# A hybrid diffusion layer: normed activations kept in DRAM as f32 rows and split again on reload, their block sums made at other times, query columns first

## The chip, the cores and the metric

The kernel runs on one core of a Trainium2 chip. The metric is device time in microseconds (us) of one execution. The engines are called as the profile calls them: PE (TensorE matmul) with PEld (its weight loads), DVE (VectorE), ACT (ScalarE), POOL (GpSimd) and SP (SyncE, which issues most DMAs here); ACT issues some stores too.

## The reference

One layer over 2048 latent tokens (a 32x64 grid) and 256 context tokens, width 1024, in f32:

```python
h_lat = _rmsnorm(x, norm_g) * (1.0 + scale) + shift      # ctx in the same way with shift_c, scale_c
na_q, na_k, na_v, na_g, r_q, r_k, r_v, r_g = _split_proj(h_lat @ w_in)      # 8 groups of 512 columns
# the context tokens go through the same weights
o_na  = neighbourhood attention, 8 heads of 64, 8x16 window plus all context keys, one softmax
y_na  = o_na * silu(na_g)
o_ret = bidirectional retention, 4 heads of 128, chunks of 128, states started from the context
y_ret = head_rmsnorm(o_ret) * silu(r_g)
x = x + gate * (concat([y_na, y_ret]) @ w_out)
return _rmsnorm(x, final_norm_g)
```

Below, h is the normed and modulated input of the projection, `h_lat` or `h_ctx`.

## The kernel before

f32 products are made on PE from pairs: each operand is split into `hi` (a cast to fp32r by ACT) and `lo` (the rest, a subtraction on DVE or POOL), and three matmuls (hi·hi, hi·lo, lo·hi) are added up in PSUM. This holds for h and for the weights. A weight group is 256 columns of `w_in`: two raw halves `st` of 128x1024, split by `w_split` into `whi` and `wlo`, for which the pool `wa` has two buffers of each.

h lies transposed in SBUF, in four latent blocks of 512 tokens and a context block of 256: `blk[b]` is a pair (hi, lo). Blocks 0 and 1 are in the pool `hx`, 2 and 3 in `hy`, the context in `cp` (`chi`, `clo`). SBUF doesn't hold all of h besides what later stages need, so blocks are written to DRAM (`hS`) and read back.

The work goes by in stages. Times are microseconds from the start of the span in the profiled execution:

- 0 to 163: x and the ada weights are loaded and the modulation made. Then `window(b)` for the five blocks: the NA keys of the block (`u_k`, PE line L354) are projected while a list of numbers, `PLAN`, interleaves the preparation of the following blocks. `prep_ab` makes raw h in place (`raw[i]`, 256 tokens each), `prep_hl` splits it.
- 163 to 197: six context units (four of `CTXU`, two of `u_v`), each of 48 matmuls of 256 columns (L365). Ahead of each a weight group is split.
- 197 to 244.6, values 1: eight `u_v` units for blocks 0 and 1. At every fifth `yield` of the units a step of `h_sums` runs.
- 244.6 to 368.7, Strassen 1 (L626): for blocks 0 and 1 the columns of `SETS` (two gate groups of each head group, `SETS` 1536, 1792, 3584, 3840, and the NA queries 0 and 256) by Strassen's form, seven products instead of eight, 12 matmuls of 512 columns each. It needs sums of h blocks, the tiles `T` from `h_sums`, and sums of weight blocks from `w_sums`. `w_set` is one column group in four steps; after each step, `hooks` and what is left of the weight sums (`mine`, `ahead`) are called.
- 368.7 to 423.7, values 2: `u_v` for blocks 3 and 2, which are reloaded from `hS`, with `h_sums` for this pair.
- 423.7 to 557.2, Strassen 2 with the products `wo_mul` of the output weights (tile `g`, stored to `woS`).
- 557.2 to 1050: more projections (retention values, keys, queries), from 592 as fill between the neighbourhood attention tiles; blocks 0 and 1 are reloaded meanwhile through the list `dmas`, one entry for one step of the fill.
- 1050 to 1391: the rest of the retention and the output projection.

Each engine takes its instructions in the order in which the program writes them, and so do the DMA queues of SP and ACT. Order is set by the Python code alone: who writes a step at which yield. `h_sums` has ten steps: `first`, `second` and `third` (two each, on 128x1024 pairs) and `fourth` (four, on 128x512). In `first` DVE subtracts hi parts, POOL lo parts (`e`), DVE adds both, ACT casts and DVE makes the low part. `spill_step` writes a piece of 512 KB of hi or lo to `hS`: 32 pieces, 16 of them in windows 2 and 3 on SP and 16 in Strassen 1 through `hooks`.

Of the kernel before, what the change touches and what calls it, by code (L numbers as in the profile page):

```python
# [18 lines left out]
P = 128  # L19
# [63 lines left out]
def hybrid_kernel(ctx: ExitStack, tc: tile.TileContext, a: dict, out: bass.AP):  # L83
# [15 lines left out]
    hS = [[dram.tile([P, KC * 512], F32, name=f"hS{b}_{hl}") for hl in range(2)] for b in range(4)]  # L99
# [146 lines left out]

    def prep_first(k):
        for i in range(2):
# [17 lines left out]
    def prep_hl(i, u):  # L266
        hi, lo = sub_dst(i)
        x, ks = raw[i][u], slice(u * KH, (u + 1) * KH)
        nc.scalar.copy(hi[:, ks, :], x)
        eng = nc.vector if LOV[i] >> u & 1 else nc.gpsimd  # L270
        eng.tensor_tensor(lo[:, ks, :], x, f(hi[:, ks, :]), ALU.subtract)  # L271
# [199 lines left out]
    SETS = (1536, 1792, 3584, 3840, 0, 256)  # L471
# [10 lines left out]
    spill = [(b, hl, k) for b in (2, 3, 0, 1) for hl in range(2) for k in range(0, KC, 2)]  # L482

    def spill_step():
        if spill:
            b, hl, k = spill.pop(0)
            nc.sync.dma_start(hS[b][hl][:, k * 512:(k + 2) * 512], f(blk[b][hl])[:, k:k + 2, :].rearrange("p k t -> p (k t)"))

    def window(b):
        units = [u_k(w01, 512 + 256 * g, ct, b) for g in range(2) for ct in range(2)]  # L490
        left = [KC] * 4
        for n, u in enumerate(STEPS if b == 0 else [u for u in range(4) for _ in range(KC)]):
            if b == 4 and n == 16:
                wr.append(w_split(wr[2]))
            next(units[u])
            left[u] -= 1
            run_acts(32 * b + n)
            if b in (2, 3) and n % 4 == 3:
                spill_step()
            if not left[u]:  # L500
                for _ in units[u]:
                    pass
                tick()
# [4 lines left out]
    def reload_parts(b):  # L508
        blk[b] = (hx.tile([P, KC, 512], F32R, name="hhi"), hx.tile([P, KC, 512], F32R, name="hlo"))
        return [(f(blk[b][hl])[:, k:k + 2, :].rearrange("p k t -> p (k t)"), hS[b][hl][:, k * 512:(k + 2) * 512])  # L510
                for k in range(0, KC, 2) for hl in range(2)]

    def h_sums(T, A, B):
# [42 lines left out]
        def fourth(k):  # L556
            if k == 0:
                tile_(1, "hhi")
                T.extend(tl[n] for n in (1, 3, 2, 4))
                tl["o"] = env["st"].tile([P, 2, 512], F32, name="o3", bufs=1)  # L560
            d = tl["o"][:, k % 2, :]
# [46 lines left out]
    def plain_next(res):  # L608
        def p1():
            res.append(w_split(wcur.pop(0), lo=1))  # L610

        return [None, p1, None, None, None, None]

    def w_set(c0, W, T, A, B, mine, ahead, hooks):
# [18 lines left out]
        def fin(o, ct, b):  # L633
# [5 lines left out]
            g = f(o)[:, 1, :]  # L639
# [4 lines left out]
        def step(n):  # L644
            tick()
            for fn in mine[4 + n:5 + n] + ahead[n:n + 1]:
                if fn:
                    fn()
            if hooks:
                for h in hooks.pop(0):  # L650
                    h()
# [21 lines left out]
        od, xd = out_tile()  # L673
# [3 lines left out]
        fin(od, 1, B)  # L677
# [38 lines left out]
    def unit(g, nsp=0):  # L716
        for _ in g:
            pass
        tick()
        for _ in range(nsp):  # L720
            spill_step()
# [10 lines left out]
    def values(ws, bb, hs, hook):  # L732
        vu = [(w, c0, tp) for w, c0 in zip(ws, (1024, 1280)) for b in bb for tp in (2 * b, 2 * b + 1)]
        y = 0
        for n, (w, c0, tp) in enumerate(vu):
            for _ in u_v(w, c0, tp):
                y += 1
                if hs and y % 5 == 0:
                    hs.pop(0)()
            tick()  # L740
            if n == 4:
                W, mine = w_sums(wcur.pop(0))
            if n > 3 and n < 7:
                mine[n - 4]()
            if n in hook:
                hook[n]()
        while hs:
            hs.pop(0)()
        mine[3]()
        return W, mine  # L750

    load_w()
    w0 = wr[3]
    for c0, u in CTXU:
# [8 lines left out]
    T = []  # L763
    W, mine = values((w0, w1), (0, 1), h_sums(T, 0, 1), {})
    wo_open()

# [4 lines left out]
    hooks = [[spill_step] if n < 16 else [] for n in range(24)]  # L771
# [3 lines left out]
    hooks[21].insert(0, lambda: take(2))  # L775
    mid = []
    strassen(T, 0, 1, W, mine, hooks, mid)
    w0, w1 = mid + [w_split(wcur.pop(0), lo=1)]
    load_w()
    load_w()  # L780
    T = []
    W, mine = values((w0, w1), (3, 2), h_sums(T, 2, 3), {1: lambda: wo_gate(7), 7: wo_row})
# [36 lines left out]
    def reload(b):  # L819
        for d in reload_parts(b):  # L820
            dmas.extend([None, None, d])

# [75 lines left out]
    def fill(n):  # L898
        for _ in range(n):
            if dmas:  # L900
                d = dmas.pop(0)
                if d:
# [643 lines left out]
```

## Time and profile before

Three runs took 1393.6, 1394.55 and 1390.81 us, the median is 1393.6. The profiled execution took 1392.92 us, its span is 1391.1 us, and the mean clock granted to PE was 0.984 of the full one.

| engine | busy us | share of span | instructions |
|---|---|---|---|
| PE | 1323.0 | 95% | 8236 |
| DVE | 840.3 | 60% | 1434 |
| POOL | 627.1 | 45% | 585 |
| ACT | 591.0 | 42% | 1239 |

The DMA moved 295.64 MB, 196.57 read and 97.52 written in HBM.

A row of the timeline reads: start and duration in us, engine, line of the kernel, operation, output and input tile, shape, count, and in brackets the idle time before it and what ended it. A row of waits reads: engine, operation and line that waited, what it waited for, us in total, times, the longest. A row of the windows has the busy time (and count) of PE, PEld, DVE, ACT and POOL in a stretch, the granted clock, the DMA's share and its GB/s.

### The profile page before, as it was taken

Reading aid. Unit: us, or ns where it says so; the run is one execution under the profiler, and the core shown is the slowest. Engines: PE = TensorE matmul, PEld = TensorE weight load, DVE = VectorE, ACT = ScalarE, POOL = GpSimd, SP = SyncE. Lnnn points to the kernel's source line nnn. Section 1 sums busy time; section 2 is a strip of 40 time slices with the busy share of each in tenths; the row PEclk is TensorE's granted clock in tenths of the full one; section 3 lists DMA queues with packets and bytes.
Section 4 is the critical chain, followed back from the end, with each engine's and each line's share of the span. In section 5 each row is a group of like instructions: output and inputs, shape, how many; then the busy total and the mean of one; then the engine's idle time right before and its main releaser. Section 6 shows DMA issues by size and latency. Waiting matters only on the chain.

```text
span 1391.1 us, 23111 instructions
## 1 busy us (share of the span) xinstructions
PE 1323.0 (95%) x8236; PEld 1157.6 (83%) x8236; DVE 840.3 (60%) x1434; ACT 591.0 (42%) x1239; POOL 627.1 (45%) x585
## 2 busy tenths in 40 slices
PE   6989999899998999899999999999999899999997
PEld 2477999688886777898899899889999789888886
DVE  5787247565676465377766777776663634344445
ACT  4454332333323334265555545456652234433332
POOL 4452434445426556255445434465433145454342
PEclk9999999999989999999999999999999999999999
DMA  9547864596975657976686899967627888555533
GB/s 310 176 166 273 287 193 111 150 351 215 349 222 145 210 189 248 297 200 185 171 225 176 214 262 271 258 181 207 174 87 249 261 289 276 184 169 167 159 114 129
DMA packets 231765, 295.64 MB, mean 213 GB/s; under 512 B 17633, under 2 KB 172385, under 8 KB 230626
## 3 DMA queue, kind: packets, MB, share of 16 engines
q1 hardware_dynamic: 200322, 237.79, 57.9%
q10 hardware_dynamic: 31328, 56.37, 11.3%
q8 instruction: 66, 1.08, 0.3%
q14 instruction: 49, 0.40, 0.1%
HBM read 196.57 MB, written 97.52 MB: 211 GB/s over the span
## 4 chain that ended last, share of the span: by engine, by line
PE 46%; DVE 4%; DMA 2%; ACT 2%; issue 1%; POOL 1%; SPq 0%; ACTq 0%; POOLq 0%; DVEq 0%
PE mm L1390 11%; PE mm L365 10%; PE sS L950 5%; PE mm L354 4%; PE tr L977 3%; PE po L998 3%; PE tr L979 2%; PE mm L1113 2%; PE po L1000 2%; DMA v<-rvS 1%; PE mm L1302 1%; PE mm L1301 1%; PE mm L1300 1%; PE mm L1281 1%; DVE xt L1358 1%
## 5 line engine op out<-in xcount | busy, mean ns | idle before, releaser
L365 PE MATMUL mm<-whi,hhi 128*128 128x256 f32 x768 | 227.1, 296 | 6.3 <-ACT o L440 5.8
L365 PE MATMUL mm<-whi,hlo 128*128 128x256 f32 x768 | 219.6, 286 | 3.3 <-DMA hlo<-hS 3.3
L365 PE MATMUL mm<-wlo,hhi 128*128 128x256 f32 x768 | 219.0, 285 | 0.0
L981 ACT CAST pt<-tr 128x640 fp32r<-128x640 f32 (+1 forms) x128 | 95.6, 747 | 169.6 <-PE tr L979 168.3
L987 DVE TENSOR_TENSOR pt<-tr,pt 128x640 fp32r<-128x640 f32 (+1 forms) x128 | 113.9, 890 | 76.9 <-ACT pt L981 75.6
L365 PEld LDWEIGHTS mm<-whi,hhi 128*128 128x128 f32 x768 | 148.6, 194 | 7.1 <-ACT o L440 6.0
L970 POOL TENSOR_SCALAR sp<-sp,stt 128x640 f32<-128x640 f32 (+2 forms) x128 | 103.0, 807 | 112.8 <-DVE stt L969 71.8
L365 PEld LDWEIGHTS mm<-whi,hlo 128*128 128x128 f32 x768 | 148.9, 194 | 4.4 <-DMA hlo<-hS 4.3
L365 PEld LDWEIGHTS mm<-wlo,hhi 128*128 128x128 f32 x768 | 148.4, 193 | 0.0
L959 DVE CUSTOM_DVE_ANT_0 sp<-sS,nb 128x640 f32<-128x640 f32 (+2 forms) x128 | 105.5, 824 | 29.3 <-PE sS L950 22.3
L964 ACT ACTIVATE sp<-sp,stt 128x640 f32<-128x640 f32 (+2 forms) x128 | 107.4, 839 | 18.9 <-DVE stt L959 17.8
L338 POOL TENSOR_TENSOR wlo<-st,whi 128x256 fp32r<-128x256 f32 (+1 forms) x79 | 83.7, 1073 | 68.8 <-ACT whi L336 67.1
L354 PE MATMUL mm<-hhi,whi 128*128 128x512 f32 x256 | 107.6, 420 | 0.0
L354 PE MATMUL mm<-hlo,whi 128*128 128x512 f32 x256 | 101.8, 398 | 5.4 <-DVE hlo L271 2.3
L950 PE MATMUL sS<-k,q 128*128 128x256 f32 (+3 forms) x512 | 98.8, 315 | 5.2 <-DVE stt L959 4.9
L354 PE MATMUL mm<-hhi,wlo 128*128 128x512 f32 x256 | 101.8, 398 | 0.2 <-DVE wlo L338 0.2
L626 PE MATMUL mm<-hhi,whi 128*128 128x512 f32 x336 | 98.4, 395 | 1.2 <-POOL whi L580 1.0
L1390 PE MATMUL mm<-wor,y 128*128 128x512 f32 x384 | 95.6, 398 | 1.0 <-DVE xt L1399 1.0
L1399 DVE TENSOR_TENSOR xt<-mm,xt 128x512 f32<-128x512 f32 x64 | 43.8, 686 | 86.1 <-PE mm L1390 86.1
L950 PEld LDWEIGHTS sS<-k,q 128*128 128x128 f32 x512 | 82.9, 188 | 11.6 <-DVE stt L959 7.7
L1390 PE MATMUL mm<-won,y 128*128 128x512 f32 x336 | 89.9, 406 | 0.0
L1390 PEld LDWEIGHTS mm<-wor,y 128*128 128x128 f32 x384 | 69.9, 188 | 17.1 <-issue 3.5
(254 smaller groups left out, 3098.3 us busy)
## 6 DMA issues: line engine op xcount, KB each, us to landing
st<-in_w_in_dram SPq DMA_DIRECT2D x64, 512.0 KB
q<-qS SPq DMA_DIRECT2D x64, 256.0 KB
k<-kS SPq DMA_DIRECT2D x16, 576.0 KB
kS<-o SPq DMA_DIRECT2D x16, 512.0 KB
hS<-hhi SPq DMA_DIRECT2D x16, 512.0 KB
hS<-hlo SPq DMA_DIRECT2D x16, 512.0 KB
vB<-o SPq DMA_DIRECT2D x64, 128.0 KB
qS<-o ACTq DMA_DIRECT2D x16, 512.0 KB
```

The lines of the kernel that those rows point to most:

```text
L338: eng.tensor_tensor(l, r, f(h), ALU.subtract)
L354: nc.tensor.matmul(pm[:, :n], ww[:, k, cs], h[:, k, :], start=(k == 0 and i == 0), stop=(k == KC - 1 and i == 2))
L365: nc.tensor.matmul(pm[:, t * WG:(t + 1) * WG], h[:, k, o:o + P], ww[:, k, :], start=(k == 0 and i == 0), stop=(k == KC - 1 and i == 2))
L626: nc.tensor.matmul(pm, ww[:, k, :], hh[:, k, :], start=(k == 0 and i == 0), stop=(k == KH - 1 and i == 2))
L950: nc.tensor.matmul(o, hd["q"][i][:, hl, j * P:(j + 1) * P], k, start=(hl == 0), stop=(hl == 1))
L959: nc.vector.tensor_tensor_reduce(T["sp"][:, :n], T["s"], nbz[big][:, o:o + n], -1.0, 3e38, ALU.add, ALU.min, T["st"][:, 0:1])
L964: nc.scalar.activation(sp[:, :n], sp[:, :n], AF.Exp, bias=st[:, 0:1], scale=-1.0, accum_out=st[:, 1:2])
L970: nc.gpsimd.tensor_scalar(sp[:, :n], sp[:, :n], st[:, 2:3], 0.0, ALU.mult, ALU.add)
L981: nc.scalar.copy(pt[:, :ng_ + 2, 0, :], tr[:, :ng_ + 2, :])
L987: nc.vector.tensor_tensor(pt[:, :n, 1, :], tr[:, :n, :], f(pt)[:, :n, 0, :], ALU.subtract)
L1390: nc.tensor.matmul(pm, yy[:, k, :], ww[:, k, sl], start=(k == 0 and i == 0), stop=(k == 3 and i == 2))
L1399: nc.vector.tensor_tensor(xts[t][:, sl], pm, xts[t][:, sl], ALU.add)
```

## The change

`hS` holds raw h, f32, one copy (8 MB) instead of hi and lo (16 MB). It is written in the windows from the raw tiles, one piece at every odd step. On reload a block is the raw rows in the `lo` tile, and `re_split` makes `hi` (ACT) and then `lo` in place (DVE or POOL). In Strassen 1 nothing is stored to `hS` any more. In the attention the splits of blocks 0 and 1 stand in `dmas` as calls.

For the first pair `h_sums` stays (its `fourth` with a tile `e` made on POOL), but its steps begin in the context units: `pump` calls one step at every eighth yield, which is the last yield of a unit, ahead of the unit's evacuation. For the second pair `h_sums_raw` makes the sums from raw rows as far as it can, with the splits between them: `open_b` in the sixth group of Strassen 1, nine steps at every fourth yield of values 2. In values 2 each block is used with both weight groups before the next (before: each weight group with both blocks), the second group is split after unit 0, and the weight sums are made after units 5 to 7 (in values 1 after 3 to 5). In `SETS` the two query groups come first; a gate group takes one `o` tile fewer.

```diff
-    hS = [[dram.tile([P, KC * 512], F32, name=f"hS{b}_{hl}") for hl in range(2)] for b in range(4)]
+    hS = [dram.tile([P, KC, 512], F32, name=f"hS{b}") for b in range(4)]
...
+    def spill_step():
+        if spill:
+            i, u = spill.pop(0)
+            o = i % 2 * 256
+            nc.sync.dma_start(hS[i // 2][:, u * KH:(u + 1) * KH, o:o + 256], raw[i][u])
...
-    SETS = (1536, 1792, 3584, 3840, 0, 256)
+    SETS = (0, 256, 1536, 1792, 3584, 3840)
...
-            if b in (2, 3) and n % 4 == 3:
+            if n % 2:
                 spill_step()
...
+        return [(f(blk[b][1])[:, k:k + 2, :], hS[b][:, k:k + 2, :]) for k in (0, 4, 2, 6)]
+
+    def re_split(b, ks, eng):
+        hi, lo = blk[b]
+        nc.scalar.copy(hi[:, ks, :], f(lo)[:, ks, :])
+        eng.tensor_tensor(lo[:, ks, :], f(lo)[:, ks, :], f(hi)[:, ks, :], ALU.subtract)
...
+        def open_b():
+            tile_(0, "hhi", F32)
+            for c in range(2):
+                V.tensor_tensor(d(c), lb[:, pairs(c + 2), :], lb[:, pairs(c), :], ALU.subtract)
+            for n in (0, 2, 1, 3):
+                re_split(B, pairs(n), (V, G)[n // 2])
...
+        def raw_a(m):
+            for n in (m, m + 2):
+                re_split(A, pairs(n), (V, G)[n // 2])
+            low(4, m, d(m), (G, V)[m])
...
+        return open_b, [a, b, lambda: first(0), lambda: first(1), c_, lambda: raw_a(0), lambda: raw_a(1), lambda: last(0), lambda: last(1)]
...
-            V(d, d, bl[:, k, :], ALU.add)
-            V(d, d, al[:, k, :], ALU.subtract)
+            V(d, d, e, ALU.add)
...
-    def unit(g, nsp=0):
+    pump = dict(y=0, every=8, q=[])
+
+    def unit(g):
         for _ in g:
-            pass
+            pump["y"] += 1
+            if pump["q"] and pump["y"] % pump["every"] == 0:
+                pump["q"].pop(0)()
...
+    pump["q"] = h_sums(T, 0, 1)
     for c0, u in CTXU:
         wn = w_split(wcur.pop(0), lo=1)
...
+    W, mine = values(vunits([(mid, 1024, 3), (w1, 1280, 3), (mid, 1024, 2), (w1, 1280, 2)]),
+                     {0: [lambda: w1.append(w_split(wcur.pop(0), lo=1)), load_w, load_w], 1: [lambda: wo_gate(7)], 7: [wo_row]}, 5)
...
+        dmas.extend([None] * 4)
+        dmas.extend(lambda k=k: re_split(b, slice(k, k + 1), nc.gpsimd) for k in (0, 1, 4, 5, 2, 3, 6, 7))
```

How this moves instructions is shown at three places. In the rows a line number is that of the kernel named, so the same operation has another number after the change. The first place is ACT in the context units, before; `whi` is a weight group's cast, `o<-mm` the evacuation of a unit:

```order
L336 CAST whi<-st 128x1024 x2
L434 ACTIVATE o<-mm 128x512
L336 CAST whi<-st 128x1024 x2
L434 ACTIVATE o<-mm 128x512
L150 DMA rkS_77<-o 128x2x256
L336 CAST whi<-st 128x1024 x2
L440 COPY o<-mm 128x512
```

And after:

```order
L348 CAST whi<-st 128x1024 x2
L599 CAST hlo<-hhi 128x1024
L446 ACTIVATE o<-mm 128x512
L348 CAST whi<-st 128x1024 x2
L599 CAST hlo<-hhi 128x1024
L446 ACTIVATE o<-mm 128x512
L150 DMA rkS_77<-o 128x2x256
L348 CAST whi<-st 128x1024 x2
L599 CAST hhi<-hhi 128x1024
L452 COPY o<-mm 128x512
```

The cast of a block sum (L599) now stands ahead of each evacuation, and so ahead of the next weight group's casts.

The second place is SP in windows 2 and 3, before; `kS` are stored keys, `in_ctxT_dram` is the context's load:

```order
L150 DMA kS_64<-o 256x1x512
L487 DMA hS_0_91<-hhi 128x1024 x2
L150 DMA kS_61<-o 256x1x512
L487 DMA hS_0_91<-hhi 128x1024
L176 DMA st<-in_ctxT_dram 128x4x256 x2
```

And after:

```order
L253 DMA hS_89<-hhi 128x4x256 x3
L150 DMA kS_64<-o 256x1x512
L150 DMA kS_61<-o 256x1x512
L253 DMA hS_90<-chi 128x4x256 x2
L176 DMA st<-in_ctxT_dram 128x4x256 x2
L150 DMA kS_62<-o 256x1x512
```

The two pieces of raw h in `chi` (tokens 1536 to 1791) are stored ahead of the context's load.

The third place is DVE at the end of Strassen 1, before; L669 to L675 are the last sums of `w_set`, L636 the low part of a query tile, L338 that of a weight group, L533 to L525 steps of `h_sums`:

```order
L669 TENSOR_TENSOR o_3022<-mm,o_3022 128x512
L636 SCALAR_TENSOR_TENSOR o<-o 128x512
L674 TENSOR_TENSOR o_3022<-mm,o_3022 128x512
L675 TENSOR_TENSOR o<-mm,e 128x512
L636 SCALAR_TENSOR_TENSOR o_3022<-o_3022 128x512
L636 SCALAR_TENSOR_TENSOR o<-o 128x512
L338 TENSOR_TENSOR wlo<-st,whi 128x1024
L533 TENSOR_TENSOR hhi<-hhi 128x1024
L535 TENSOR_TENSOR hhi<-hhi 128x1024
L525 TENSOR_TENSOR hlo<-hhi,hlo 128x1024
```

And after, where L742 to L748 are those last sums, L544 and L520 are `open_b`, L537, L558, L564 and L565 the steps `a`, `b` and `first`, and L416 the evacuation of a value unit:

```order
L742 TENSOR_TENSOR o_2995<-mm,o_2995 128x512
L544 TENSOR_TENSOR hhi<-hlo 128x1024 x2
L520 TENSOR_TENSOR hlo<-hlo,hhi 128x1024 x2
L747 TENSOR_TENSOR o_2995<-mm,o_2995 128x512
L748 TENSOR_TENSOR o<-mm,e 128x512
L537 TENSOR_TENSOR hlo<-hhi,hlo 128x1024
L558 TENSOR_TENSOR hhi<-hhi,hlo 128x1024 x2
L416 TENSOR_TENSOR o<-mm,o 128x4x128
L350 TENSOR_TENSOR wlo<-st,whi 128x1024
L564 TENSOR_TENSOR o_3152<-hhi,hlo 128x1024
L565 TENSOR_TENSOR o_3152<-o_3152,hlo 128x1024
```

The splits and sums of the second pair stand ahead of the last two sums of Strassen 1 and of the second weight group.

More of the change, by code (lines that the diff above doesn't have):

```diff
@@ L245, in ab @@
         return scl[u][:, q, s:s + 1], mod[u][:, 0, q, s:s + 1]
+    spill = []
+    def spill_step():
[3 more added lines that the diff above has]
+            nc.sync.dma_start(hS[i // 2][:, u * KH:(u + 1) * KH, o:o + 256], raw[i][u])
     def prep_first(k):
+        if k == KC - 1:
+            spill.extend((i, u) for i in range(2) for u in range(2))
         for i in range(2):
@@ L269, in prep_hl @@
         nc.scalar.copy(hi[:, ks, :], x)
+        if i < 8:
+            spill.append((i, u))
         eng = nc.vector if LOV[i] >> u & 1 else nc.gpsimd
@@ L480, in load_w @@
             wcur.append(w_raw(wseq.pop(0)))
[L482 to L487, printed above, removed]
     def window(b):
@@ L769, in take, with take_a @@
             nc.sync.dma_start(*d)
-    hooks = [[spill_step] if n < 16 else [] for n in range(24)]
+    T2, raws = [], []
+    def take_a():
+        take(2)
+        raws.extend(h_sums_raw(T2, 2, 3))
+    hooks = [[] for n in range(24)]
     for k in range(7):
```

111 lines of the change are left out of this document (72 added, 39 removed).

## The prediction

> **What bounds the kernel now.** I read the page first: busy shares, then the granted clock.
>
> ```profile
> PE 1323.0 (95%) x8236; PEld 1157.6 (83%) x8236; DVE 840.3 (60%) x1434; ACT 591.0 (42%) x1239; POOL 627.1 (45%) x585
> PEclk9999999999989999999999999999999999999999
> ```
>
> TensorE (PE) is busy 95% of 1391.1 us and nearly always at full clock, and the change keeps its matmuls. So it can only move the stalls. Those I read in PE's waits, then stage by stage in the windows (columns: stretch, length, busy time and count of PE, PEld, DVE, ACT, POOL, clock, DMA share, GB/s).
>
> ```profile
> PE mm L626 <- ACT wlo L579: 8.4, 3, 4.8
> PE mm L365 <- ACT o L440: 5.8, 1, 5.8
> PE mm L626 <- POOL wlo L580: 4.3, 6, 1.3
> PE mm L365 <- DMA hlo<-hS: 3.3, 4, 0.9
> ...
> 163.00:197.00 34.00, 33.36 (x277) 32.96 (x276) 12.45 (x7) 13.02 (x16) 20.59 (x9) 1.00 0.74 237
> 197.00:244.60 47.60, 47.60 (x399) 47.60 (x398) 35.65 (x29) 12.23 (x18) 16.55 (x9) 1.00 0.45 113
> 244.60:368.70 124.10, 119.68 (x506) 96.52 (x505) 75.68 (x91) 43.18 (x75) 60.98 (x43) 0.97 0.75 251
> 368.70:423.70 55.00, 51.19 (x385) 49.67 (x385) 41.46 (x34) 14.31 (x19) 22.80 (x10) 0.91 0.77 254
> 423.70:557.20 133.50, 124.00 (x510) 96.05 (x509) 78.05 (x94) 52.00 (x90) 81.22 (x59) 0.97 0.63 203
> 557.20:592.00 34.80, 29.00 (x226) 28.54 (x224) 11.21 (x17) 10.21 (x17) 9.70 (x12) 0.90 0.96 296
> ...
> 275.00:365.00 90.00, 90.00 (x391) 73.17 (x389) 54.33 (x62) 32.74 (x56) 45.78 (x32) 1.00 0.82 282
> ```
>
> The stages are the six context units, values 1, Strassen 1, values 2, Strassen 2, and the first units after it. The last row is undisturbed: 90/391 = 0.2302 us per 512-column matmul; values 1 gives 47.6/399 = 0.1193 per 256-column one. By the code a Strassen stage has 504 (116.0 us), a values stage 384 (45.8 us), a context unit 48 (5.7 us; 5.76 with its change of unit). So Strassen 1 loses 8.1, values 2 9.2, Strassen 2 17.5, and the six context units nothing. The losses are these:
>
> ```profile
> 253.38 0.50 PE L626 MATMUL mm<-hhi,wlo 128*128 128x512 f32 x1 [3.13 <-ACT wlo L579]
> 381.45 0.39 PE L365 MATMUL mm<-whi,hlo 128*128 128x256 f32 x1 [0.91 <-DMA hlo<-hS]
> 254.00:261.00 7.00, 5.71 (x15) 4.40 (x15) 2.38 (x5) 2.91 (x6) 7.00 (x6) 0.51 0.79 191
> 383.60:394.00 10.40, 8.41 (x34) 7.54 (x35) 8.04 (x8) 2.57 (x3) 0.00 (x0) 0.51 1.07 374
> 424.90:441.80 16.90, 11.20 (x36) 8.15 (x37) 0.80 0.61 152
> ```
>
> Stall A: Strassen 1 starts on weight sums that stand behind the h sums on DVE and ACT, then runs 7 us at clock 0.51. Stall B: values 2 starves on reloaded blocks, with 10.4 us at 0.51. Stall C: by 441.8 Strassen 2 has done 36 matmuls (8.3 us of work) in 16.9 us (so the last row, L626 alone): 8.6 lost, the same way as A.
>
> **The change, part by part. Context units.** The first pair's sums now start here, one step at each unit's end, ahead of the unit's evacuation on ACT. The rows of before:
>
> ```profile
> 160.78 8.06 POOL L338 TENSOR_TENSOR wlo<-st,whi 128x1024 fp32r<-128x1024 f32 x3 [10.73 <-ACT whi L336]
> 169.94 0.60 ACT L434 ACTIVATE o<-mm 128x512 f32<-128x512 f32 x1 [4.63 <-PE mm L365]
> 170.44 1.98 ACT L336 CAST whi<-st 128x1024 fp32r<-128x1024 f32 x2
> 171.55 2.40 POOL L338 TENSOR_TENSOR wlo<-st,whi 128x1024 fp32r<-128x1024 f32 x1 [2.71 <-ACT whi L336]
> 172.51 2.52 DVE L338 TENSOR_TENSOR wlo<-st,whi 128x1024 fp32r<-128x1024 f32 x1 [5.92 <-ACT whi L336]
> ...
> 214.16 2.40 POOL L525 TENSOR_TENSOR hhi<-hhi 128x1024 fp32r<-128x1024 f32 x1 [16.61 <-ACT hhi L524]
> 215.21 2.44 DVE L543 TENSOR_TENSOR hhi<-hhi 128x1024 f32<-128x1024 f32 x1
> 217.68 1.23 DVE L544 TENSOR_TENSOR hhi<-hhi,hlo 128x1024 f32<-128x1024 f32 x1
> ...
> L524 ACT CAST hlo<-hhi 128x1024 fp32r<-128x1024 f32 x4 | 4.2, 1048 | 14.4 <-DVE hhi L553 8.0 <-DVE hhi L535 6.4
> ```
>
> Today a weight group is split while a unit computes: ACT evacuates (0.60), casts two halves (1.98), and POOL and DVE subtract one each (2.40 and 1.23). All that fits into 5.76 us. The DVE rows also show that POOL and DVE exclude each other where both read SBUF: the subtraction that takes 1.23 alone took 2.44 beside POOL's 2.40 and ended 1.09 after it (217.65 against 216.56). Likewise at 172.51.
>
> After the change the chain of one period is: POOL's wlo ends; DVE's wlo gets the port (1.1); POOL's e subtraction (2.4); DVE's sum of both (1.2); the ACT cast (1.05); the evacuation (0.6); the next group's first cast (1.0); POOL's next wlo (2.4). A delayed e or a second DVE operation before the sum adds 1.2: 10.9 in all. The two steps of `second` have no e but two DVE sums in row, and POOL's low part before its wlo: 1.2+1.2+1.05+0.6+1.0 beside 2.4+2.4 and port turns, 9.5. PE needs a new group every 5.76. POOL's three wlo end at 168.84; from there the groups for units 2 to 5 are ready at 177.65 (no delay in the first period), 188.55, 198.0 and 207.5. Unit 2 was due at 174.4: stalls of 3.3, then 188.55-183.4 = 5.1, 198.0-194.3 = 3.7 and 207.5-203.8 = 3.7, together 15.8. At half clock a unit lasts longer, but only the last shows, since the chain covers the others. I take **+16**; lower bound +8 (period 8.7 without port turns), upper +18.
>
> The Trainium skill ("SBUF — State Buffer", Who interferes with whom) says that such a pair of operations excludes each other for a whole instruction, by order of issue; the rows above agree, and by ports without it this term would be the lower bound, +8. It speaks against moving these sums here.
>
> **Strassen 1.** With the sums begun 60 us sooner, only four steps stand in values 1, and the weight sums come at unit 3 instead of 4 on a DVE with less in front of it. A goes. The 8.1 held 3.13 and neighbours plus half clock, all of it: **-7.5** (bounds -8 and -5, if a weight sum is still short).
>
> **Values 2 and the start of Strassen 2.** Half the bytes come back, but each pair of 128x1024 now needs a cast (1.05) and a subtraction (1.23 DVE or 2.40 POOL) before it may be used, and the next pair's sums go on the same engines at once.
>
> ```profile
> 367.47 0.68 DVE L669 TENSOR_TENSOR o<-mm,o 128x512 f32<-128x512 f32 x1
> 374.09 2.41 POOL L338 TENSOR_TENSOR wlo<-st,whi 128x1024 fp32r<-128x1024 f32 x1 [10.52 <-ACT whi L336]
> 376.46 6.68 POOL L534 TENSOR_TENSOR hhi<-hlo 128x1024 f32<-128x1024 f32 x2
> 377.51 3.42 DVE L533 TENSOR_TENSOR hhi<-hhi 128x1024 f32<-128x1024 f32 x1
> ```
>
> `open_b` stands behind L669's successor on DVE, so its two differences start at about 368.2 and its four splits follow, alternating with POOL: the first low pair is ready at about 374.1, the second at 377.6, and unit 0, which was due at 368.7, ends at about 385 instead of 374.5. The split of the second weight group then comes at about 392.6 and unit 2 ends at 398.5, unit 3 at 404.3. Unit 4 needs the other block's splits. Ahead of them on the shared port stand, with themselves, 18 DVE operations of 1.22 and 8 of POOL of 2.4: 41.2 us from 368, and some 5 for hand-overs: 414. I let unit 4 end at 424 and the stage at 441 (three more units of 5.76). Then C is gone, since only `last` is open. Before had 36 matmuls of Strassen 2 done at 441.8; after has them at 441.3+36x0.2302 = 449.6. That is 7.8, of which I take **+6**, since some of the 5 us for hand-overs may not show. Lower bound -12 (DVE and POOL overlap as 377.51 does not: B and C vanish, less unit 0's 5.4, the four splits that it needs in any case), upper +10.
>
> **Order of sets, gates last.** After Strassen 2 ACT stood on the store of the `g` tile and the evacuation came late:
>
> ```profile
> 568.58 0.62 ACT L709 CAST g<-wraw 128x512 fp32r<-128x512 f32 x1 [6.73 <-DMA woS<-g]
> 571.40:578.30 6.90, 3.57 (x17) 3.57 (x18) 1.04 (x2) 3.06 (x4) 4.98 (x4) 0.51 0.91 324
> ```
>
> The 5.8 on L440 and 6.9 us at 0.51 (3.4) hang on a store. The gates write half the bytes of the q groups, but their stores now come last; the queue ahead of `g` may be shorter or not: **-1** (bounds -8, all of it gone, and +1).
>
> **Windows and stores.** In Strassen 1 eight of the old spill's 16 MB fall away; I price that at nothing, since 275-365 runs undisturbed with the DMA at 0.82. The windows get the f32 spill, 16 transfers on SP, on every second step.
>
> ```profile
> 112.14 2.14 SPq L176 DMA_DIRECT2D st<-in_ctxT_dram  x2
> 113.89 2.94 DVE L262 TENSOR_SCALAR chi<-chi,mods 128x256 f32<-128x256 f32 x2
> 119.35 2.00 ACT L198 ACTIVATE st<-st 128x1024 f32<-128x1024 f32 x2
> ```
>
> Two pieces of `chi` now stand ahead of the context load. The second is scaled only at 116.8 (113.89+2.94), so the load is issued near 117.5 instead of 112.14. Its squares began at 119.35, of which some 3 us were slack: about 2 later, and the column sums that the last window needs with them: **+2** (bounds 0 and 5, with a half-clock stretch).
>
> **Attention.** Blocks 0 and 1 are split by 16 casts on ACT and 16 subtractions on POOL, two per tile.
>
> ```profile
> 843.75 0.80 POOL L970 TENSOR_SCALAR sp<-sp,stt 128x640 f32<-128x640 f32 x1 [3.59 <-DMA vc<-vS]
> 846.68 0.60 PE L977 MATMUL tr<-ident,sp 128*96 128x128 f32 x4
> 800.00:840.00 40.00, 39.61 (x283) 36.61 (x282) 30.74 (x70) 19.88 (x41) 16.96 (x18) 1.00 0.95 261
> ```
>
> POOL ends at 844.55 and PE reads at 846.68: 2.1 of slack. Two half-size subtractions are about 2.4 (one 128x1024 in the rows above), so 0.3 for each of eight tiles shows unless less DMA (0.95 busy here) helps: **+1** (-2 to +4).
>
> The sum: 2+16-7.5+6-1+1 = +16.5. The profiled execution took 1392.92, 0.7 below the median 1393.6 of three, so 1392.9+16.5 = **1409**. Less than 0.3% (4.2 us) counts as no change.
>
> **Rivals.** *Faster.* DVE and POOL overlap better than the chain says, or the context chain is shortened because POOL starts e before wlo's input is there: context +8, A -8, values 2 and C -12, E -3, windows +2: -13, **1380**. It decides if the context units lose under 8 us and values 2 end before 420. For it: POOL is only 45% busy, and B and C (17.8) really go. Against: POOL and DVE take the port in turn at 172.51, 215.21 and 377.51.
>
> *No change.* The context term comes as priced but values 2 lands between, near -8: 1392.9+16.5-14 = **1395**. For it: values 2's bounds are far apart. Against: the unit-0 start needs four splits whatever the port does.
>
> *Half clock.* The stalls are as long as those that brought 0.51 rows. If the last two context units and units 4 to 6 of values 2 run whole at 0.51, that adds 5.7+8 to the forecast: **1423**. For it: stalls of 3.13 and 0.91x4 sufficed. Against: the chain covers slow matmuls elsewhere. The Trainium skill ("TensorE: Matmul & The Clock Gate", Part 1: The HAM clock gate) has PE halved after an idle window of about 3.4 us; most stalls here are at that size.
>
> *No hold.* The relief does nothing: A stays because the weight sums on POOL still come late: 1409+7.5 = **1416**.
>
> **How the numbers follow.** Forecast 0.50, half clock 0.12, A stays 0.10: slower 0.72. Faster 0.19, no change 0.09. The range runs from 1388, between faster and no change, to 1425, just over the half-clock case: outside are most of the faster case's 0.19 and almost nothing above. The forecast's own range is 1400 to 1418.
>
> **What would show it.** Right: PE waits for wlo in the context units, 12 us or more over four stalls, with ACT's evacuation behind a cast of the sums; no stall at the start of Strassen 1; values 2 over 65 us, its waits on hlo by DVE or POOL rather than on a DMA; a short start of Strassen 2; PE at L209's successor in the last window later by about 2. Wrong: context units within 5 us of 34.6 (DVE and POOL overlap), or values 2 at 50 us. A queue that I have not seen filling, above all the stores on ACT behind a cast that waits, would move the gates' end more than -1.

## The result and the profile after

Four runs of the changed kernel took 1406.78, 1406.02, 1416.1 and 1407.39 us, median 1407.09; the kernel before 1393.17. The ratio is 1.0116, 95% interval 1.0072 to 1.016: slower by 14 us, against 16.5 forecast. The profiled execution has a span of 1405.0 us against 1391.1.

The page of the changed kernel, busy times and clock:

```profile
PE 1325.7 (94%) x8236; PEld 1161.0 (83%) x8236; DVE 833.4 (59%) x1422; ACT 606.8 (43%) x1261; POOL 654.2 (47%) x603
PEclk9999989999989999999999999999999999999999
```

PE does the same 8236 matmuls in a span that is 13.9 longer. POOL and ACT are busy 27 and 16 us longer, DVE 7 less. PE's waits show where it stands now (`L377` is the matmul line of the value and context units, `L350` the weight split, `L519` and `L520` the cast and subtraction of `re_split`):

```profile
PE mm L377 <- POOL wlo L350: 9.2, 5, 2.0
...
PE mm L377 <- DVE hlo L520: 5.7, 4, 1.7
...
PE mm L377 <- ACT hhi L519: 4.6, 2, 3.8
PE mm L209 <- DVE st L203: 4.3, 2, 4.2
...
PE tr L1061 <- POOL sp L1054: 3.4, 7, 1.2
```

The 8.4 us in which L626 waited for ACT's weight sums are gone but for 0.5; the waits for reloads are gone too. In their place stand waits for weight groups in the context units, for the split of reloaded blocks, and for the context's column sums (L209). By stage (windows of the changed kernel: context units, values 1, Strassen 1, values 2, Strassen 2, the next 192 matmuls):

```profile
166.20:217.40 51.20, 41.95 (x290) 40.71 (x290) 34.11 (x20) 17.70 (x21) 26.28 (x11) 0.87 0.48 154
217.40:263.50 46.10, 46.10 (x386) 46.10 (x385) 19.65 (x24) 9.89 (x17) 19.54 (x13) 1.00 0.65 167
263.50:381.10 117.60, 116.83 (x506) 94.60 (x504) 71.69 (x84) 41.40 (x71) 55.86 (x39) 1.00 0.56 189
381.10:449.40 68.30, 54.69 (x387) 52.31 (x388) 43.66 (x33) 24.25 (x32) 30.32 (x12) 0.88 0.57 155
449.40:570.80 121.40, 118.79 (x507) 94.46 (x506) 71.52 (x87) 48.74 (x84) 75.59 (x54) 1.00 0.62 212
570.80:599.20 28.40, 24.66 (x193) 24.45 (x192) 5.40 (x9) 6.57 (x10) 8.32 (x9) 0.94 0.91 262
```

The same cuts (first matmul of each stage to first of the next) in the profiles of all kernels, in us. "Windows" is the time up to the first context unit, "rest" all after the 192 matmuls behind Strassen 2.

| kernel | windows | context units | values 1 | Strassen 1 | values 2 | Strassen 2 | next 192 | rest | span | median of runs |
|---|---|---|---|---|---|---|---|---|---|---|
| before | 162.8 | 35.7 | 46.1 | 124.2 | 56.2 | 132.3 | 30.4 | 803.4 | 1391.1 | 1393.2 |
| after | 166.2 | 51.2 | 46.1 | 117.6 | 68.3 | 121.4 | 28.4 | 805.8 | 1405.0 | 1407.1 |
| e7_before_pump | 164.6 | 52.0 | 46.1 | 116.6 | 56.2 | 132.5 | 30.2 | 802.0 | 1400.2 | 1401.5 |
| e1_late | 169.1 | 34.6 | 46.1 | 126.6 | 69.5 | 123.5 | 30.0 | 803.8 | 1403.2 | 1407.0 |
| e2_mid | 167.7 | 34.5 | 46.1 | 128.0 | 68.6 | 123.0 | 29.5 | 805.1 | 1402.5 | 1404.0 |
| e3_half | 166.3 | 42.6 | 46.1 | 117.6 | 68.4 | 121.8 | 28.3 | 809.6 | 1400.7 | 1403.7 |
| e4_dve | 169.9 | 42.5 | 46.0 | 117.7 | 68.3 | 122.5 | 28.2 | 808.8 | 1403.9 | 1404.6 |
| e5_spill | 165.2 | 51.1 | 46.1 | 117.7 | 68.3 | 121.7 | 28.9 | 808.0 | 1407.0 | 1406.4 |
| e6_vals_dve | 171.0 | 49.7 | 46.1 | 117.6 | 62.2 | 123.2 | 28.9 | 806.9 | 1405.6 | 1405.5 |
| e8_before_sets | 164.0 | 35.6 | 46.1 | 122.9 | 54.1 | 134.3 | 28.4 | 801.0 | 1386.4 | 1389.7 |
| e9_attn | 168.1 | 49.7 | 46.0 | 117.7 | 68.2 | 121.3 | 30.2 | 803.9 | 1405.1 | 1407.4 |
| e12_mid_dve | 162.6 | 34.5 | 46.1 | 120.2 | 68.3 | 123.8 | 29.5 | 804.6 | 1389.6 | 1392.5 |
| e13_mid_dve_vals | 163.2 | 34.5 | 46.1 | 119.5 | 61.7 | 122.9 | 30.5 | 806.4 | 1384.8 | 1387.4 |
| e14_before_mid | 164.1 | 35.5 | 46.0 | 122.2 | 52.9 | 128.8 | 26.8 | 803.9 | 1380.2 | 1383.7 |

A stage repeats within about 2 us between executions in which its code and what precedes it are the same (context units 49.7 to 51.2, the next 192 matmuls 28.4 to 30.2), except the windows (up to 5 us, from the first loads on) and the rest (up to 6). So the stages are compared by profile, the whole by the medians. "Values 2" here holds four matmuls of the output weights too, about 1.3 us ahead of Strassen 2.

The context units, the first group's `wlo` and then one period of the chain in the changed kernel (timeline of POOL, DVE and ACT, put in order of time):

```profile
167.85 2.38 POOL L350 TENSOR_TENSOR wlo<-st,whi 128x1024 fp32r<-128x1024 f32 x1 [0.94 <-ACT whi L348]
...
178.58 2.35 POOL L350 TENSOR_TENSOR wlo<-st,whi 128x1024 fp32r<-128x1024 f32 x1 [5.00 <-ACT whi L348]
180.89 3.36 POOL L609 TENSOR_TENSOR hhi<-hlo 128x1024 f32<-128x1024 f32 x1
181.93 3.40 DVE L608 TENSOR_TENSOR hhi<-hhi 128x1024 f32<-128x1024 f32 x1
185.43 1.23 DVE L610 TENSOR_TENSOR hhi<-hhi 128x1024 f32<-128x1024 f32 x1
186.69 1.05 ACT L599 CAST hlo<-hhi 128x1024 fp32r<-128x1024 f32 x1 [7.25 <-DVE hhi L610]
187.64 0.59 ACT L446 ACTIVATE o<-mm 128x512 f32<-128x512 f32 x1
188.13 1.98 ACT L348 CAST whi<-st 128x1024 fp32r<-128x1024 f32 x2
189.24 2.35 POOL L350 TENSOR_TENSOR wlo<-st,whi 128x1024 fp32r<-128x1024 f32 x1 [5.00 <-ACT whi L348]
```

From POOL's `wlo` to its next `wlo` 10.66 us go by, while PE needs a group every 5.76. Each step is the one priced: POOL, then the port's turn (of DVE and POOL one waits for the other: 3.36 and 3.40 where their bare times are 2.4 and 1.22), DVE, cast, evacuation, cast. ACT idles 7.25 us ahead of the cast, with the evacuation and the weight casts behind it in its queue; POOL idles 5.00. PE's waits from 166 to 220:

```profile
PE mm L377 <- POOL wlo L350: 7.7, 4, 2.0
PE mm L377 <- ACT whi L348: 1.6, 2, 1.0
```

Four of the five waits for `wlo` on the page above lie here; the fifth is in values 2.

### The profile page after: what moved, and what is told of

Same layout as the page of the kernel before. It is cut to its first block, busy times and chain, and to the rows that moved or that the text cites. A ratio compares the mean times of both kernels' runs of the same rounds, so it can differ in the third digit from the quotient of the medians.

```text
span 1405.0 us, 23114 instructions
## 1 busy us (share of the span) xinstructions
PE 1325.7 (94%) x8236; PEld 1161.0 (83%) x8236; DVE 833.4 (59%) x1422; ACT 606.8 (43%) x1261; POOL 654.2 (47%) x603
## 2 busy tenths in 40 slices
DMA packets 233301, 278.86 MB, mean 198 GB/s; under 512 B 17121, under 2 KB 180065, under 8 KB 232162
## 4 chain that ended last, share of the span: by engine, by line
PE 65%; DMA 8%; DVE 8%; POOL 7%; issue 6%; ACT 4%; SPq 2%; ACTq 1%; POOLq 0%; DVEq 0%
PE mm L377 16%; PE mm L1474 11%; PE mm L702 10%; PE mm L366 7%; PE sS L1034 4%; PE tr L1061 3%; PE po L1082 3%; PE mm L1197 2%; DMA hlo<-hS 2%; PE tr L1063 2%; PE po L1084 1%; DMA woS<-g 1%; PE mm L314 1%; POOL hlo L520 1%; DMA v<-rvS 1%
## 5 line engine op out<-in xcount | busy, mean ns | idle before, releaser
L377 PE MATMUL mm<-whi,hhi 128*128 128x256 f32 x768 | 227.6, 296 | 8.3 <-ACT hhi L519 4.6
L377 PE MATMUL mm<-whi,hlo 128*128 128x256 f32 x768 | 220.5, 287 | 8.2 <-DVE hlo L520 5.7
L377 PE MATMUL mm<-wlo,hhi 128*128 128x256 f32 x768 | 219.9, 286 | 1.6 <-POOL wlo L350 1.6
L377 PEld LDWEIGHTS mm<-whi,hlo 128*128 128x128 f32 x768 | 149.7, 195 | 9.6 <-DVE hlo L520 6.6
L377 PEld LDWEIGHTS mm<-whi,hhi 128*128 128x128 f32 x768 | 149.4, 194 | 9.2 <-ACT hhi L519 5.2
L377 PEld LDWEIGHTS mm<-wlo,hhi 128*128 128x128 f32 x768 | 149.3, 194 | 1.8 <-POOL wlo L350 1.8
L350 POOL TENSOR_TENSOR wlo<-st,whi 128x256 fp32r<-128x256 f32 (+1 forms) x79 | 83.6, 1069 | 59.2 <-ACT whi L348 48.3
L656 POOL TENSOR_TENSOR wlo<-st,wlo 128x512 fp32r<-128x512 f32 x36 | 51.5, 1432 | 79.7 <-ACT wlo L655 74.9
## 6 DMA issues: line engine op xcount, KB each, us to landing
vB<-o SPq DMA_DIRECT2D x64, 128.0 KB, 2.1
```

The source lines that it names most:

```text
L350: eng.tensor_tensor(l, r, f(h), ALU.subtract)
L377: nc.tensor.matmul(pm[:, t * WG:(t + 1) * WG], h[:, k, o:o + P], ww[:, k, :], start=(k == 0 and i == 0), stop=(k == KC - 1 and i == 2))
L656: nc.gpsimd.tensor_tensor(t[:, 1], r, f(t)[:, 0], ALU.subtract)
```

## Experiments: the first pair's sums

**e7_before_pump**: this part of the change alone, in the kernel before.

```diff
+            pump["y"] += 1
+            if pump["q"] and pump["y"] % 8 == 0:
+                pump["q"].pop(0)()
...
+    pump["q"] = h_sums(T, 0, 1)      # ahead of the context units; the last four at every eighth yield of values 1
```

> The kernel before with one part of the change alone: the first pair's sums begin in the context units, one step at each unit's end, the last four at every eighth yield of values 1 (there POOL makes no e in the fourth step). Theory (this part does the same here as in the changed kernel): context units 35.7 to about 51, Strassen 1 124.2 to 118 to 121, the rest as before: 1392+15.5-6.5 to -3.5 = 1401 to 1404. Rival (the stalls in the context units need the changed kernel's stores and loads beside them): the context units stay under 42 and the kernel gets faster, 1390.

Measured: 1401.46 against 1393.64, ratio 1.0051 (1.0036 to 1.0067), as expected. Windows of this kernel, context units and Strassen 1:

```profile
164.60:216.60 52.00, 40.59 (x291) 38.84 (x290) 33.10 (x20) 17.69 (x21) 29.09 (x12) 0.90 0.49 156
262.70:379.30 116.60, 116.60 (x506) 94.76 (x505) 68.82 (x81) 40.76 (x69) 54.79 (x39) 1.00 0.73 252
```

52.0 for 35.7 and 116.6 for 124.2: +16.3 and -7.6, with the old stores and loads around. The loss of the context units and the end of stall A come from this one part, and together they are 8 of the 14 us.

**e1_late** and **e2_mid**: the changed kernel with the sums begun later.

```diff
-    pump["q"] = h_sums(T, 0, 1)                              # ahead of the context units
+    pump.update(y=0, every=5, q=h_sums(T, 0, 1))             # e1: ahead of values 1, weight sums after unit 4
+    pump.update(y=0, every=5, q=h_sums(T, 0, 1))             # e2: ahead of the last two context units
```

> The first pair's sums start with values 1 again, one step at every fifth yield, weight sums after unit 4; all else as in the changed kernel. Theory (the sums' chain through POOL, DVE and ACT holds back the weight groups): the six context units fall from 49.8 to about 34.6 us, and stall A at the start of Strassen 1 comes back, 117.6 to about 124; together -9 on 1407, so 1398. Rival 1 (the context units lose to the SP stores and loads that now stand there, not to the sums): they stay near 49 us and the time near 1407. Rival 2 (A went because of the new order of the sets, not because the sums began sooner): Strassen 1 stays at 117.6 and the time is about 1392.

> The first pair's sums start at the fifth of the six context units, behind the last weight split, one step at every fifth yield; all else as in the changed kernel. Theory: no weight group stands behind a sum, so the context units take 34.6 to 36 us; the sums still begin 12 us sooner than before, so most of stall A stays away (Strassen 1 117.6 to 120): 1407-15 = 1392, between 1390 and 1395. Rival (only a start four units earlier keeps A away): Strassen 1 back at 124, 1398.

Measured: 1407.03 (ratio to before 1.0116, 1.0097 to 1.0136) and 1404.04 (1.009, 1.0073 to 1.0106). The stages went as the theory says in the context units (34.6, 34.5). Strassen 1 (e1, then e2) took longer than the 124.2 of before, where it was to be 124 in e1 and 117.6 to 120 in e2:

```profile
249.80:376.40 126.60, 119.61 (x506) 95.98 (x504) 80.16 (x94) 44.51 (x77) 63.47 (x45) 0.97 0.58 191
...
248.30:376.30 128.00, 120.80 (x507) 96.26 (x505) 80.45 (x93) 44.67 (x77) 63.01 (x44) 0.97 0.61 199
```

So e1's total was missed by 9 and e2's by 12. In e2 the ten steps take from 195.5 to 253, though they were written much sooner:

```profile
249.28 1.29 POOL L638 TENSOR_TENSOR e<-hlo 128x512 f32<-128x512 f32 x1
250.61 0.69 DVE L640 TENSOR_TENSOR o<-o,e 128x512 f32<-128x512 f32 x1 [3.69 <-POOL e L638]
```

DVE waits 3.69 us for a POOL operation of 1.29, which stands behind two low parts of the weight sums in POOL's queue, and the evacuations and the other weight sums wait behind DVE. Here the sums are slow because they go to and fro between engines that wait for each other (e12 below takes that away); where they begin decides which stage pays. Context units and Strassen 1 together took 159.9 before, 168.8 after, 161.2 and 162.5 here, and would take 150.6 without stalls (34.6+116.0). The rest of e1's miss lies in stages that it did not change (windows 169.1, Strassen 2 123.5); why these were longer in it stays open.

**e3_half**: casts and low parts one step after the additions. **e4_dve**: POOL left out of the weight splits and of the first four steps of the sums, so nearly out of the context units (3.03 us are left).

```diff
-            nc.scalar.copy(t[:, 0, ks, :], d)                             # e3, in cut()
-            (V if key == 3 else G)(t[:, 1, ks, :], d, f(t)[:, 0, ks, :], ALU.subtract)
+            held.append(...)                                              # e3: the two lines above, run at the next step's start
...
-        wn = w_split(wcur.pop(0), lo=1)                                   # e4, the split of w1 likewise
+        wn = w_split(wcur.pop(0), lo=0)
-            G(e, bl[:, kt, :], bl[:, ks, :], ALU.subtract)
+            V(e, bl[:, kt, :], bl[:, ks, :], ALU.subtract)
-            (V if key == 3 else G)(t[:, 1, ks, :], d, f(t)[:, 0, ks, :], ALU.subtract)   # e4
+            (V if key in (2, 3) else G)(t[:, 1, ks, :], d, f(t)[:, 0, ks, :], ALU.subtract)
```

> As the changed kernel, but the cast and the low part of each sum are issued one step later than its additions, so that no ACT cast waits for additions of its own period. Theory with port turns (POOL and DVE exclude each other): a period still has two POOL operations of 2.4 and two to four of DVE of 1.22, 8.5+9.7+7.3+8.5 = 34 us for four periods instead of 40.2 measured; the context units fall by 6, from 49.8 to about 44, and the time to 1401. Rival (only the order on ACT, the cast ahead of evacuation and weight casts, holds it back): the stalls all but vanish, context units 36 to 38 us, 1394.

> As the changed kernel, but POOL does nothing in the context units: both halves of each weight group's low part, the difference e and the low part of the second step are made by DVE. Theory with port turns: DVE runs alone at 1.22 each, a period is 1.0+1.0+1.2+3.7+1.05+0.6 = 8.5 us in the first two and 7.3 in the next two instead of 10.7 and 9.4, so the context units fall by about 8, from 49.8 to about 42, and the time to 1399, though DVE gets 2 to 3 more operations for each period. Rival without port turns (the DVE durations of 2.5 to 3.4 have another cause, and POOL's help is real): the chain gets two more DVE operations in row and one POOL operation less, no gain or a loss of up to 5 us, 1407 to 1412.

Measured: 1403.66 and 1404.56, where 1401 and 1399 were expected: the totals fell by 3.4 and 2.5 us only, though the context units did what was forecast. In the profiles the rest took 3 to 4 us more (809.6, 808.8) and in e4 the windows too (169.9), which is within their spread; whether the gain is lost there or only covered stays open. The context units in the windows of the two:

```profile
166.30:208.90 42.60, 38.25 (x290) 37.64 (x289) 40.24 (x20) 17.19 (x21) 28.30 (x10) 0.92 0.59 181
...
169.90:212.40 42.50, 38.80 (x291) 37.78 (x290) 33.27 (x29) 17.71 (x21) 3.03 (x2) 0.92 0.59 185
```

42.6 and 42.5 us, where 44 and 42 were expected by port turns and 36 to 38 or no gain by the rivals. The order of the casts and low parts is therefore part of it (e3 gains 8.6 by breaking it) but not all: with the order broken the two engines still can't deliver. And taking POOL's work away gains 8.7 us although DVE then runs 29 operations instead of 20 there; its busy time even falls from 34.1 to 33.3, since its operations no longer wait for POOL's. In e4 a sum takes DVE's bare time:

```profile
182.14 1.22 DVE L608 TENSOR_TENSOR hhi<-hhi 128x1024 f32<-128x1024 f32 x1
183.28 1.22 DVE L609 TENSOR_TENSOR hhi<-hlo 128x1024 f32<-128x1024 f32 x1
184.53 1.23 DVE L610 TENSOR_TENSOR hhi<-hhi 128x1024 f32<-128x1024 f32 x1
```

3.6 us for all three, against 5.8 with POOL's help (180.89 to 186.66 above).

## Experiments: the other terms

**e5_spill**: `chi` and `clo` stored behind the context's load.

```diff
-        if spill:
+        if spill and (spill[0][0] < 6 or 8 in raw):
```

> As the changed kernel, but the pieces of raw h in chi and clo are stored behind the context's load instead of ahead of it. Theory (that load stands on SP behind a store that waits for the piece to be scaled): the load is issued 4 to 5 us sooner relative to the scaling, PE's wait for the context's column sums (L209) falls from 4.2 to about 1.2 us, with the half clock behind it 3 to 5 us less, time about 1403. Rival (the late start is spread of the first 30 us, which moves by 2 us from run to run): the wait stays over 3 us and the time at 1407.

Measured: 1406.36, where 1403 was expected. The changed kernel's timeline (SP, ACT, PE), then the wait in this kernel:

```profile
112.01 4.16 SPq L253 DMA_DIRECT2D hS<-chi  x2
116.27 1.55 SPq L176 DMA_DIRECT2D st<-in_ctxT_dram  x2
121.46 1.06 ACT L198 ACTIVATE st<-st 128x1024 f32<-128x1024 f32 x1 [3.10 <-DMA st<-in_ctxT_dram]
126.34 0.85 PE L209 MATMUL mm<-one,st 128*128 128x1 f32 x4 [4.17 <-DVE st L203]
```

```profile
PE mm L209 <- DVE st L203: 1.4, 2, 1.2
```

The wait is 1.2 again, and the cause is shown. In this total it is not to be seen, since the windows' end moves by 3 to 5 us with the first loads alone. Over all profiles with the load behind the stores the windows end at 166.2 to 171.0 (seven, mean 168.3), with it free at 162.6 to 165.2 (seven, mean 163.8), so the 3 to 5 expected stand in the stage.

**e6_vals_dve**: no POOL in values 2 but for the weight sums (3.85 us).

```diff
-                re_split(B, pairs(n), (V, G)[n // 2])
+                re_split(B, pairs(n), V)          # the low parts and the second weight group likewise
```

> As the changed kernel, but in values 2 every subtraction of the reload's splits, of the second pair's low parts and of the second weight group is made by DVE; POOL does none. Theory with port turns: 26 DVE operations of 1.22 (31.7 us) take the place of 18 of 1.22 and 8 of POOL of 2.4 (41.2 us), so unit 4's splits come 5 to 9 us sooner and values 2 fall from 68.3 to 59 to 63 us; time about 1400. Rival (order and waits for the casts hold it, POOL is a real help): values 2 stay at 68 or grow by up to 5, 1407 to 1412.

Measured: 1405.51, values 2 in its window:

```profile
384.40:446.60 62.20, 53.68 (x389) 51.76 (x389) 41.86 (x42) 24.41 (x32) 3.85 (x3) 0.89 0.62 172
```

62.2 for 68.3 (59 to 63 expected), again with DVE busy less (41.9 for 43.7) for nine more operations. The total missed by 5, since Strassen 2 gave 1.8 back and this execution's windows ended at 171.0.

**e8_before_sets**: only the order of the sets, in the kernel before.

```diff
-    SETS = (1536, 1792, 3584, 3840, 0, 256)
+    SETS = (0, 256, 1536, 1792, 3584, 3840)
```

> The kernel before with only the order of the sets changed: the two query groups first, gates last, with one o tile fewer for a gate. Theory: it is worth the 2 us that the first units after Strassen 2 lost less (30.4 against 28.4), 1391, within 1388 to 1394; stalls A, B and C stay, Strassen 1 at 124 and Strassen 2 at 132. Rival: the order of the sets, not the early sums of raw rows, cleared the start of Strassen 2; then that stage falls to about 122 and the time to 1382.

Measured: 1389.69, ratio 0.9985 (0.9973 to 0.9997), so 2.6 us faster (interval 0.4 to 3.8). The next 192 matmuls take 28.4, as in the changed kernel; but that stage alone doesn't show it, since with the new order it took 26.8 to 30.5 in the other profiles and with the old one 30.2 and 30.4. Strassen 2 stays long (134.3). So the order is worth some 2 us by the medians, and stall C ended in the changed kernel for another reason: the sums of the second pair are ready when values 2 end. The first 17 us of Strassen 2 in the changed kernel have no gap:

```profile
449.40:466.40 17.00, 17.00 (x74) 13.71 (x73) 10.87 (x11) 6.89 (x13) 11.69 (x9) 1.00 0.40 119
```

74 matmuls where the kernel before had 36.

**e9_attn**: the subtractions of the re-split left out in the attention, so that the low parts hold raw rows there.

```diff
-        dmas.extend(lambda k=k: re_split(b, slice(k, k + 1), nc.gpsimd) for k in ...)
+        dmas.extend(lambda k=k: nc.scalar.copy(blk[b][0][:, k:k + 1, :], f(blk[b][1])[:, k:k + 1, :]) for k in ...)
```

> As the changed kernel, but the 16 subtractions on POOL that split blocks 0 and 1 again during the attention are left out (the casts on ACT stay; the low parts then hold raw rows, so the output is not the reference's). The rest of the kernel after the first 192 matmuls behind Strassen 2 took 803.4 and 801.0 us with the old reload and 804 to 810 with the new one. Theory (POOL's subtractions make its step of the attention tiles late): the rest falls by 2 to 5, to 802 to 805, time 1403. Rival (the casts on ACT, or the spread of single executions): the rest stays at 804 to 810, 1406 to 1407.

Measured: 1407.37, the rest 803.9. Its wait in the attention:

```profile
PE tr L1061 <- POOL sp L1054: 1.6, 4, 0.6
```

The wait falls from 3.4 to 1.6, the value of before, so 1.8 us are shown to come from POOL's subtractions. The rest took 801.0 to 803.9 in four kernels with the old reload and 803.8 to 809.6 in nine with the full new one, on average 4.0 more. That it fell here by no more than its spread, and the median not at all where 1403 was expected, leaves the other 2 us of these 4 open.

## Experiments: versions with repairs

**e12_mid_dve**, **e13_mid_dve_vals**, **e14_before_mid**: the sums from the fifth context unit on, all on DVE, casts one step later. e12 is the changed kernel with this and e5's order, e13 adds e6; e14 is the kernel before with this (all on DVE and casts one step later for both pairs, the first pair's sums from the fifth context unit on, its weight sums after unit 3) and e8's order.

```diff
+    pump.update(y=0, every=5, q=h_sums(T, 0, 1))      # ahead of the last two context units
-            G(e, ...)
+            V(e, ...)                                  # also for the low parts
+            held.append(...)                           # as in e3
```

> As the changed kernel, but the first pair's sums start at the fifth context unit (one step at every fifth yield), all on DVE and each cast issued one step later, and the stores of chi and clo stand behind the context's load. Theory: with POOL out of the sums DVE needs 20 operations of 1.22 and 16 of 0.69, 35 us and some 6 for evacuations, where the same start with POOL needed 57; so the weight sums come in time. Context units 34.6, Strassen 1 117.6 to 120, first windows 3 to 5 us less: 1404-9-4, about 1391. Rival (the weight sums themselves, on POOL, are late, or DVE alone is too slow): Strassen 1 stays over 124 and the time at 1398 or more.

> The changed kernel with three repairs together: chi and clo stored behind the context's load; the first pair's sums from the fifth context unit on, all on DVE, casts one step later; values 2 with all subtractions on DVE. Theory: the repairs act in different stages and add up, 1392.5 of the first two less the 6 that values 2 fell by, plus 1 at Strassen 2: 1387, within 1384 to 1390. Rival (what one stage gains the next one waits for): 1391 or more.

> The kernel before, h kept as hi and lo, with the query groups first and both pairs' sums on DVE with casts one step later, the first pair's from the fifth context unit on with the weight sums after unit 3. Theory: Strassen 1 falls from 124 to about 120 and the order of the sets is worth 2.6; values 2, bound by the reload, stay at 54 to 56 and Strassen 2 near 130: 1392.3-2.6-4 = 1386, within 1382 to 1390. Rival (DVE alone is too slow for the second pair, whose sums cannot start early): stall C grows, 1391 or more.

Measured: e12 1392.48 (ratio to before 1.0003, 0.9991 to 1.0015), e13 1387.39 (0.9974, 0.996 to 0.9988), e14 1383.74 (0.9947, 0.9926 to 0.9968). Strassen 1 in e12, then values 2 and Strassen 2 in e14:

```profile
243.20:363.40 120.20, 117.75 (x507) 94.22 (x505) 75.26 (x88) 42.49 (x73) 57.89 (x40) 1.00 0.61 202
...
367.80:420.70 52.90, 50.15 (x390) 48.42 (x388) 43.48 (x44) 16.18 (x22) 6.92 (x4) 0.97 0.81 257
420.70:549.50 128.80, 121.97 (x506) 95.04 (x505) 77.61 (x97) 51.00 (x88) 74.55 (x55) 0.99 0.66 216
```

The totals came close to what was expected (1391, 1387, 1386); e14's Strassen 1 was to be 120 and took 122.2. With the sums on DVE alone and each cast one step later, the start that failed in e2 (128.0) gives 120.2, and the context units keep 34.5; which of the two does how much was not tried by itself. e14 is the fastest, 3.6 us below e13 in the medians. By stages e13's Strassen stages are 8.6 shorter (242.4 against 251.0), 5.9 of it in the second, whose sums are made early from raw rows, and its values 2 are 8.8 longer (61.7 against 52.9), where the reload has to be split again; the two cancel. The rest of e14's lead lies behind, in the next 192 matmuls and the attention (830.7 against 836.9), where it reloads hi and lo and splits nothing. No run here shows a gain from the smaller DMA traffic (278.86 MB after, 295.64 before).

## Why the prediction was right

Its sign, its size and its largest terms held; the total came 2.6 below the forecast, with misses of single terms in both directions, the largest of 4.8. By terms, from the two profiles:

| term | predicted | measured | how |
|---|---|---|---|
| windows | +2 | +3.4 | 162.8 to 166.2; PE's wait at L209 from 1.2 to 4.2 |
| context units | +16 | +15.5 | 35.7 to 51.2 |
| Strassen 1 | -7.5 | -6.6 | 124.2 to 117.6 |
| values 2 and Strassen 2 | +6 | +1.2 | 188.5 to 189.7 |
| order of sets | -1 | -2.0 | 30.4 to 28.4 |
| attention and rest | +1 | +2.4 | 803.4 to 805.8 |
| sum | +16.5 | +13.9 | 1391.1 to 1405.0 |

Context units: the period was priced at 10.9 and 9.5; between the weight casts of the changed kernel lie 10.66, 9.0 and 9.6. That the whole came so close is in part luck. The first period was priced at 8.8, without delay, and took 10.7 like the second (POOL's `wlo` ends at 170.2 and 180.9); but the group before it was ready 4.0 us after the stage's start and not 5.8. The sign that was named, 12 us or more of PE waiting for `wlo` in four stalls, was not seen: it waited 7.7 in four, and 1.6 for `whi`. The rest of the 15.5 stands in PE's busy time, 41.95 us for matmuls that take 34.6 where the stage has no stall, with a granted clock of 0.87.

Strassen 1: A went, as priced. e7 shows that it went for the reason named, the earlier sums (116.6 with this part alone), and e1 that it returns with the late start; e2 shows that beginning somewhat sooner is not enough, and e12 that there is a cheaper way.

Values 2 with the start of Strassen 2 is the term that was mis-sized, by 4.8. The port sum in it held. POOL's last split of the second block and the matmul of unit 4 that waits for it (timeline of the changed kernel):

```profile
422.39 3.33 POOL L520 TENSOR_TENSOR hlo<-hlo,hhi 128x1024 fp32r<-128x1024 f32 x1
425.77 0.39 PE L377 MATMUL mm<-whi,hlo 128*128 128x256 f32 x1 [2.59 <-POOL hlo L520]
```

The split ends at 425.7, 44.6 after the stage's first matmul; 414 from 368.7 was 45.3. The step that failed is the next: unit 4 was to end 10 us behind its splits (424), but by then it had done 19 of its 48 matmuls, on the pairs that were ready, and the next unit begins at 430.9, 5.2 behind. Unit 0 also took 11.6 (381.1 to 392.7) and not 16.3, which later waits hid. The four matmuls ahead of Strassen 2 (448.1 to 449.4) were not counted, which took 1.3 the other way. So 36 matmuls of Strassen 2 are done 76.6 after the stage began (449.4+8.3-381.1) against 73.1 before: +3.5 for the 7.8 worked out and the 6 taken. The other 2.3 came after those 36 matmuls, in a part of Strassen 2 that was priced at nothing. PE's waits for weight sums there fell from 3.7 to 2.4; the remaining 1 us and the cause of both are open. The order of the sets alone did not shorten this stage (e8).

Windows and attention lay within their bounds, on the high side; the mechanism of the one is shown (e5), of the other only the part that POOL's wait carries (e9). On the sizes of these two and of the order of sets the two profiles alone say little, since the stages differ by as much between executions; over all profiles the windows end 4.5 later (163.8 to 168.3).

Of the rivals, *faster* fell with the port: e4 and e6 gain by taking POOL away, which overlapping engines would not do. *Half clock* came only in stretches (0.87 in the context units, 0.88 in values 2) behind waits that the chains set anyway (read from the rows, not tried by itself), and Strassen 1 runs at 1.00. *No hold* fell: A went. *No change* needed values 2 and the start of Strassen 2 near -8; they came at +1.2, between it and the forecast's +6. What the Trainium skill ("SBUF — State Buffer", Who interferes with whom) says of such pairs was borne out: DVE's 3.40 beside POOL's 3.36 above, and its 1.22 without it.

## What to carry to other kernels

Moving work earlier moves its stall unless the engines have spare time there as a chain, not as a share: here POOL at 45% and DVE at 60% of the span did not help, because each step went POOL, DVE, ACT in row and ACT's queue held the next weight group behind it. Price such a move as a period, in order of the queues, and compare it with the period of the bound engine. Where two engines hold each other up, as DVE and POOL do here, giving all the subtractions to the faster one can be quicker than dividing them (e4, e6).

## What was not expected of the hardware

That DVE waits for POOL within its own recorded duration could be read from the rows of before (1.23 alone, 2.44 beside POOL). Not expected was how much: leaving POOL out lowered DVE's own busy time while DVE got more instructions (34.1 to 33.3 us with 20 and 29 operations in the context units; 43.7 to 41.9 with 33 and 42 in values 2). A share of busy time on DVE can hold a good deal of waiting.
